# A hybrid decoder layer in split float32r: token parts of 688 and 344 instead of 516 and 516 in the Strassen products of the feed-forward block

## Chip, cores and metric

The kernel runs on one core of a Trainium2 chip. The metric is the time of one execution on the device in microseconds (us). Three runs of the kernel before the change took 2125.63, 2126.91 and 2134.8 us; the median is 2126.91 us.

## What is computed

One inference step of a one-layer decoder for 1024 prompt tokens and 8 sample tokens (1032 columns in all, `TOK`), width 1024. The time mixing (RWKV-7 and gated DeltaNet) fills the first half of the run and is not touched. What follows is, cut to its core:

```python
gate_a = jax.nn.sigmoid(pg[..., :D_MODEL])
gate_b = jax.nn.sigmoid(pg[..., D_MODEL:])
mix = gate_a * (o_a.astype(act) @ w_branch_a) + gate_b * (o_b.astype(act) @ w_branch_b)
h = h + mix @ w_out
u2 = rmsnorm(h, norm_ffn)
h = h + (jax.nn.silu(u2 @ w_ffn_gate) * (u2 @ w_ffn_up)) @ w_ffn_down
h = h + jax.nn.sigmoid(rmsnorm(h, norm_ple) @ w_ple_gate) * (pe.astype(act) @ w_ple_proj)
```

Weights are 1024x1024 for `w_out`, 1024x2816 for gate and up (22 tiles of 128, `NF`), 2816x1024 for down.

## The kernel before

Activations lie transposed: 128 features on the partitions, tokens in the columns. Every large product is made in float32r with both operands split in two: `x = xh + xl`, `w = wh + wl`, and for each 128x128 block of weights three products `wh*xh`, `wh*xl`, `wl*xh` (`mm`, L75). `wh` is made by ScalarE (ACT, L186), `wl` by GpSimd (POOL, L187) in `halves_of`, from raw weights that SyncE (SP) loads. `dense` takes one output tile `m`: it loads and splits the weights (`weights`) and then runs `products` over blocks of tokens, each into a PSUM tile `acc`, which `evac` reads.

`wst` holds raw weights (2 buffers), `wsp` split ones (6).

From L1497 on, the product with `wo` runs in two halves of the tokens, `t = 0` and `t = 1`, 516 tokens each, made of two quarters `QB` of 258 columns (`QW`). The evacuation adds the input (loaded into a tile `a`), stores `h` to DRAM, and `square` adds up squares: a square `c` by ACT, added to `sq` by POOL (L1458). After the last `m` the squares are summed over the partitions by two small products into `f` (L75), with `inv_rms` on VectorE (DVE) between them, which gives the norm `R` of the quarter.

Then `mixes` (L1473) scales `H` (L1482) and makes, from four quadrants (features 0 to 511 and 512 to 1023, first and second quarter of the half), the seven sums of Strassen's scheme: a sum `c` (L1490), its high part `xh` by ACT (L1492) and its low part `xl` (L1493). DVE and POOL take sums and low parts in turn. The temporaries `c` come from the same two buffers as the squares.

`strassen` (L1524) makes two output tiles of gate or up for a token half from seven products instead of eight: it loads four raw blocks of weights (`A_`, from a pool `raw` of 6 buffers), forms a sum of weights `s` for five of the seven (L1568; three on POOL, two on DVE), splits it, and multiplies by the matching sum of tokens: 12 `mm` of 258 columns per half. For the first pair of tiles (`f0 + j == 0`) gate and up run for half 0 alone and then again for half 1 (`for ts_ in ((0,), (1,))`), so their weights are loaded, summed and split twice. For the other ten pairs each split weight serves both halves. After 2, 4, 4, 4, 4, 4 tiles the down product runs (L1618), each block of 344 columns read from `h_d` into `a` (4 buffers), added (L1612) and stored back.

The pools `raw`, `sp`, `hid` of the feed-forward block are opened after `hpool.close()`, behind `mixes` of half 1:

```python
        XM.append(mixes(pool(cstk, f"xm{t}", 1, "right"), t, R))
    hpool.close()
    hstk = ExitStack()
    hp = pool(hstk, "hid")
    raw = pool(hstk, "raw", 6)
    sp = pool(hstk, "sp", 2)
```

They lie in the memory that `H`, `sq` and the halves of `mix` have left, so the first raw weights and sums of gate wait for the last use of those. A scheduler orders each engine's instructions by priorities (`tc.cur_priority`) and its own forecast of times; each engine then takes its instructions strictly in that order.

Of the kernel before, what the change touches and what calls it, by code (L numbers as in the profile page):

```python
# [58 lines left out]
def hybrid(ctx, tc, a, o):  # L59
# [120 lines left out]
    wst = pool(ctx, "wst", 2)  # L180
# [29 lines left out]
    def dense(src, nk, xh, xl, evac, blocks=range(NBLK)):  # L210

        tc.cur_priority += LATER
        wh, wl = weights(src, nk)
        tc.cur_priority -= LATER
        products(wh, wl, nk, xh, xl, evac, blocks)
# [3 lines left out]
    def products(wh, wl, nk, xh, xl, evac, blocks=range(NBLK), new=None):  # L219
        tc.cur_priority += LATER  # L220
        for b in blocks:
# [7 lines left out]
            for k in range(nk):  # L229
                mm(ps, wh[k], xh[k][:, c], start=(k == 0), stop=False)  # L230
                mm(ps, wh[k], xl[k][:, c], start=False, stop=False)
                mm(ps, wl[k], xh[k][:, c], start=False, stop=(k == nk - 1))
# [57 lines left out]
    with tc.tile_pool(name="ld", bufs=1, side="right", reuse_waits="tile") as ld, \  # L290
# [66 lines left out]
        def project(m):  # L357
            po = ld.tile([P, TOK], F32, tag="po", name="po", bufs=5)
# [1063 lines left out]

    def tile(tag, n=BW):
        return tmp.tile([P, n], F32, tag=tag, name=tag, bufs=4 if tag == "a" else 2)
# [8 lines left out]
    hpool, mstk = ExitStack(), ExitStack()  # L1433
    hq = pool(hpool, "hq", 1)
    H = [hq.tile([P, TOK], F32, name=f"H{m}") for m in range(KT)]
    mx = pool(mstk, "mx", 1)
    mh, ml = pair(mx, "mx", KT)
    for m in range(KT):
        def evac(b, ps, m=m):
            g = tile("a")  # L1440
            SP.dma_start(g, gate_d[KT + m, :, cols(b)])
            y = tile("c")
            stt(y, g, 1.0, ps, ADD, MULT)
            gtt(y, y, U[m][:, cols(b)], ADD)
            split(y, None, mh[m][:, cols(b)], ml[m][:, cols(b)])
        dense(a["wb"][m], HB, obh, obl, evac)
# [21 lines left out]
    QW = TOK // 4  # L1468
    QB = [slice(i * QW, (i + 1) * QW) for i in range(4)]
    cstk = ExitStack()  # L1470
    idr = diagonal(hq, QW)

    def mixes(pl_, t, R):  # L1473


        hi, lo = ([pl_.tile([P, 4, QW], F32R, name=f"x{q}{t}{i}") for i in range(7)] for q in "hl")
        tc.cur_priority += 2 * LATER
        for k in range(4):
            y = []
            for kk in (k, k + 4):  # L1480
                for c, r in zip(QB[2 * t:2 * t + 2], R):
                    stt(H[kk][:, c], H[kk][:, c], vc("nffn", kk), r, MULT, MULT)  # L1482
                    y.append(H[kk][:, c])
            y11, y12, y21, y22 = y
            for i, (p, q, op) in enumerate(((y11, y22, ADD), (y11, None, None), (y12, y22, SUB), (y21, y11, SUB),
                                            (y22, None, None), (y11, y12, ADD), (y21, y22, ADD))):
                e, e2 = (gtt, tt) if i % 2 else (tt, gtt)
                if op:
                    s = tile("c", QW)
# [4 lines left out]
        tc.cur_priority -= 2 * LATER  # L1494
# [3 lines left out]
    for t in range(2):  # L1498
        R = [hq.tile([P, QW], F32, name=f"R{t}{i}") for i in range(2)]
        sq = [hq.tile([P, QW], F32, tag=f"sq{i}", name="sq") for i in range(2)]  # L1500
        for m in range(KT):
            def evac(c, ps, m=m):
                i = (c.start - QB[2 * t].start) // QW
                x = tile("a", QW)
                SP.dma_start(x, a["xT"][m, :, c])
                h = H[m][:, c]
                tt(h, ps, x, ADD)
                SP.dma_start(h_d[m, :, c], h)
                square(m, c, h, sq[i], R[i], hq)
# [12 lines left out]
    sg = [hp.tile([P, TOK], F32, name=f"sg{i}") for i in range(2)]  # L1522

    def strassen(src, j, ts_, evac):  # L1524
# [3 lines left out]
        for i, q in ((0, 0), (1, 1), (1, 0), (0, 1)):  # L1528
            A_[i, q] = raw.tile([P, 4, P], F32, tag="r", name="r")
# [4 lines left out]
        def new(tag):  # L1534
            return sp.tile([P, QW], F32, tag=tag, name=tag)

        def sums(n, t, ps):
            if n == 0:
# [22 lines left out]
        for n, p, q, op, e in ((0, (0, 0), (1, 1), ADD, gtt), (3, (1, 1), None, None, None), (1, (1, 0), (1, 1), ADD, tt),  # L1561
                               (2, (0, 0), None, None, None), (4, (0, 0), (0, 1), ADD, gtt),
                               (5, (1, 0), (0, 0), SUB, tt), (6, (0, 1), (1, 1), SUB, gtt)):
# [5 lines left out]
            h, l = halves_of(s, 4)  # L1569
            for t in ts_:  # L1570
                banks.append(banks.pop(0))
                ps = banks[-1].tile([P, QW], F32, tag="acc", name="acc")
                xh_, xl_ = (x[n] for x in XM[t])
                for k in range(4):
                    mm(ps, h[:, k], xh_[:, k], start=(k == 0), stop=False)
                    mm(ps, h[:, k], xl_[:, k], start=False, stop=False)
                    mm(ps, l[:, k], xh_[:, k], start=False, stop=(k == 3))
                sums(n, t, ps)
            tc.cur_priority -= LATER

# [148 lines left out]
```

## Time and profile before

| | |
|---|---|
| median of three runs | 2126.91 us |
| the profiled execution | 2130.15 us, its span 2128.3 us |
| busy share of the span: PE, DVE, POOL, ACT | 91%, 62%, 50%, 40% |
| mean granted TensorE clock | 0.957 |
| chain that ended last | PE 62%, DVE 19%, POOL 5%, ACT 4%, DMA 4% |
| `mm` into `acc` in the chain | 53% of the span |

PE is the matrix engine's products, PEld its weight loads; DVE, ACT, POOL and SP are VectorE, ScalarE, GpSimd and SyncE. The duration of a product in a row is longer than its share of the time, since products are pipelined; what one costs is the distance from its start to the next start.

### The profile page before, as it was taken

Reading aid. Unit: us, or ns where it says so; the run is one execution under the profiler, and the core shown is the slowest. Engines: PE = TensorE matmul, PEld = TensorE weight load, DVE = VectorE, ACT = ScalarE, POOL = GpSimd, SP = SyncE. Lnnn points to the kernel's source line nnn. Section 1 sums busy time; section 2 is a strip of 40 time slices with the busy share of each in tenths; the row PEclk is TensorE's granted clock in tenths of the full one; section 3 lists DMA queues with packets and bytes.
Section 4 is the critical chain, followed back from the end, with each engine's and each line's share of the span. In section 5 each row is a group of like instructions: output and inputs, shape, how many; then the busy total and the mean of one; then the engine's idle time right before and its main releaser. Section 6 shows DMA issues by size and latency. Waiting matters only on the chain.

```text
span 2128.3 us, 40132 instructions
## 1 busy us (share of the span) xinstructions
PE 1936.3 (91%) x14676; PEld 1804.6 (85%) x14676; DVE 1328.3 (62%) x3264; ACT 856.3 (40%) x2080; POOL 1070.9 (50%) x1162
## 2 busy tenths in 40 slices
PE   6997999899899988999799908799999999999996
PEld 5987878777778868899799907699999999999995
DVE  8469756987898349636552756464463636446667
ACT  5343353555554341247423334242332414234542
POOL 5366362566563244741156559463554636455632
PEclk9999899999999999899899959999999999999998
DMA  6433332243343424554545511624335152432322
GB/s 218 143 110 106 105 106 87 83 127 94 98 126 113 147 83 122 165 154 137 167 138 168 149 35 60 214 61 147 113 96 164 61 170 79 136 110 79 94 92 96
DMA packets 215998, 252.96 MB, mean 119 GB/s; under 512 B 47960, under 2 KB 171752, under 8 KB 215800
## 3 DMA queue, kind: packets, MB, share of 16 engines
q1 hardware_dynamic: 215800, 250.39, 38.3%
q8 instruction: 115, 1.88, 0.4%
q14 instruction: 83, 0.68, 0.1%
HBM read 172.92 MB, written 77.40 MB: 118 GB/s over the span
## 4 chain that ended last, share of the span: by engine, by line
PE 62%; DVE 19%; POOL 5%; issue 5%; ACT 4%; DMA 4%; SPq 1%; DVEq 0%; ACTq 0%; POOLq 0%
PE acc L75 53%; PE f L75 3%; PE c L75 2%; POOL wl L187 2%; PE zp L75 1%; DVE GM L737 1%; DVE inv L773 1%; PE f L79 1%; DVE L L626 1%; DMA a<-h_d 1%; PE s L75 1%; POOL xl L1493 1%; PE x L75 1%; DMA ws<-in_wpg 1%; DVE LB L761 1%
## 5 line engine op out<-in xcount | busy, mean ns | idle before, releaser
L75 PE MATMUL acc<-xh,wh 128*128 128x258 f32 (+2 forms) x2360 | 733.8, 311 | 44.3 <-ACT wh L186 33.8
L75 PE MATMUL acc<-xl,wh 128*128 128x258 f32 (+2 forms) x2360 | 727.6, 308 | 1.3 <-DVE xl L253 1.3
L75 PE MATMUL acc<-xh,wl 128*128 128x258 f32 (+1 forms) x2336 | 722.5, 310 | 1.1 <-POOL wl L187 1.0
L75 PEld LDWEIGHTS acc<-xh,wh 128*128 128x128 f32 (+1 forms) x2360 | 450.5, 191 | 55.4 <-ACT wh L186 37.7
L187 POOL TENSOR_TENSOR wl<-ws,wh 128x512 fp32r<-128x512 f32 (+1 forms) x204 | 264.9, 1301 | 395.4 <-ACT wh L186 335.5
L75 PEld LDWEIGHTS acc<-xl,wh 128*128 128x128 f32 (+1 forms) x2360 | 451.5, 191 | 9.2 <-DVE xl L253 2.4
L75 PEld LDWEIGHTS acc<-xh,wl 128*128 128x128 f32 x2336 | 447.4, 192 | 8.0 <-POOL wl L187 2.2
L187 POOL TENSOR_TENSOR wl<-s,wh 128x512 fp32r<-128x512 f32 x120 | 157.1, 1313 | 154.6 <-ACT wh L186 149.5
L186 ACT ACTIVATE wh<-ws 128x512 fp32r<-128x512 f32 (+1 forms) x204 | 126.2, 620 | 206.2 <-PE acc L75 140.2
L75 PE MATMUL acc<-hidh,wh 128*128 128x344 f32 x528 | 165.9, 320 | 8.8 <-DVE a L1612 8.8
L75 PE MATMUL acc<-hidl,wh 128*128 128x344 f32 x528 | 168.4, 321 | 0.0
L75 PE MATMUL acc<-hidh,wl 128*128 128x344 f32 x528 | 167.3, 319 | 0.0
L1612 DVE TENSOR_TENSOR a<-a,acc 128x344 f32<-128x344 f32 x120 | 60.8, 512 | 148.4 <-DMA a<-h_d 92.4
L186 ACT ACTIVATE wh<-s 128x512 fp32r<-128x512 f32 x120 | 75.6, 630 | 142.1 <-PE acc L75 122.8
L75 PEld LDWEIGHTS acc<-hidh,wh 128*128 128x128 f32 x528 | 98.7, 188 | 10.3 <-DVE a L1612 5.6
L75 PEld LDWEIGHTS acc<-hidl,wh 128*128 128x128 f32 x528 | 99.0, 188 | 0.0
L75 PEld LDWEIGHTS acc<-hidh,wl 128*128 128x128 f32 x528 | 98.9, 188 | 0.0
L1568 POOL TENSOR_TENSOR s<-r 128x512 f32<-128x512 f32 x72 | 96.6, 1344 | 4.6
L187 POOL TENSOR_TENSOR wl<-r,wh 128x512 fp32r<-128x512 f32 x48 | 63.9, 1331 | 61.5 <-ACT wh L186 57.0
L492 POOL TENSOR_TENSOR cy<-cy,cu 128x344 f32<-128x344 f32 x72 | 68.6, 953 | 48.8 <-ACT cu L491 42.7
L75 PE MATMUL acc<-mxh,wh 128*128 128x258 f32 x256 | 72.7, 284 | 0.0
L75 PE MATMUL acc<-mxl,wh 128*128 128x258 f32 x256 | 72.4, 283 | 0.0
(496 smaller groups left out, 4143.5 us busy)
## 6 DMA issues: line engine op xcount, KB each, us to landing
ws<-in_win SPq DMA_DIRECT2D x92, 256.0 KB, 3.1
a<-h_d SPq DMA_DIRECT2D x120, 172.0 KB, 2.4
h_d<-a SPq DMA_DIRECT2D x120, 172.0 KB, 2.8
pa_d<-gs SPq DMA_DIRECT2D x90, 172.0 KB, 1.9
r<-in_wg SPq DMA_DIRECT2D x48, 256.0 KB, 2.7
r<-in_wu SPq DMA_DIRECT2D x48, 256.0 KB, 2.6
ws<-in_wd SPq DMA_DIRECT2D x40, 256.0 KB, 2.7
gate_d<-gs SPq DMA_DIRECT2D x48, 172.0 KB, 2.7
```

The source lines that it names most:

```text
L75: last[0] = TE.matmul(out, w, x, start=start, stop=stop).ins
L79: last[0] = TE.transpose(out, x, ident).ins
L186: act(h, s, AF.Copy)
L187: (eng or gtt)(l, s, h.bitcast(F32), SUB)
L492: gtt(y, y, u, ADD)
L626: V.tensor_tensor_scan(L[:, c * C:c * C + C], ones[:, 0:C], L[:, c * C:c * C + C], 0.0, MULT, ADD)
L737: stt(GM[:, 2 * (c + j) + h], ps[h][:, j], cvf[:, cg, h:h + 1], rwmask, MULT, MULT)
L761: V.transpose(LB[0:32, i0:i0 + 16], G2[:, :, i0:i0 + 16].rearrange("p b i -> p i b"))
L773: tt(u[:, :i], XB[:, :i, :i], LB[:, 16 + i:17 + i, 16:16 + i].to_broadcast([P, i, i]), MULT)
L1493: e2(lo[i][:, k], p, hi[i][:, k].bitcast(F32), SUB)
L1568: e(s, A_[p], A_[q], op)
L1612: tt(y, y, ps, ADD)
```

## The change

The two token parts get 688 and 344 tokens, each still of two equal blocks: 344 columns in part 0 and 172 in part 1. `H`, the norms `RN` and the halves of `mix` become one set of tiles for each part, `products` gets an offset `t0`. The sums in `mixes` get three buffers `ms` of their own, the scaling is one instruction per feature tile over the whole part, and the seven sums are made one after the other in the order in which they are used (`SIX`). The pools that Strassen uses (`sp`, `sx`, and `sg`) are opened ahead of the product with `wo`; the raw weights lie in `wst` (now 3 buffers) and `sp`. In the first pair gate takes all seven products of part 0 and then, with the same split weights, those of part 1; up is done as in the other pairs. `po` in the start goes from 5 buffers to 4, `a` from 4 to 3 before the down products and to 5 in them.

```diff
-    wst = pool(ctx, "wst", 2)
+    wst = pool(ctx, "wst", 3)
...
-            po = ld.tile([P, TOK], F32, tag="po", name="po", bufs=5)
+            po = ld.tile([P, TOK], F32, tag="po", name="po", bufs=4)
...
-        return tmp.tile([P, n], F32, tag=tag, name=tag, bufs=4 if tag == "a" else 2)
+        return tmp.tile([P, n], F32, tag=tag, name=tag, bufs=depth[0] if tag == "a" else 2)
...
+    QB = [slice(0, BW), slice(BW, 2 * BW), slice(2 * BW, 5 * BW // 2), slice(5 * BW // 2, TOK)]
+    NT_ = [2 * BW, BW]
...
+    sp, sx = pool(sstk, "sp", 2, "right"), pool(sstk, "sx", 1, "right")
+    sg = [sp.tile([P, TOK], F32, name=f"sg{i}", bufs=1) for i in range(2)]
+    SIX = (0, 3, 1, 2, 4, 5, 6)
...
-        tc.cur_priority += 2 * LATER
-        for k in range(4):
-            y = []
-            for kk in (k, k + 4):
-                for c, r in zip(QB[2 * t:2 * t + 2], R):
-                    stt(H[kk][:, c], H[kk][:, c], vc("nffn", kk), r, MULT, MULT)
...
+        tc.cur_priority += LATER
+        for m in range(KT):
+            stt(H[t][m], H[t][m], vc("nffn", m), RN[t], MULT, MULT)
+            y.append([H[t][m][:, :qw], H[t][m][:, qw:]])
+        for i in SIX:
+            for k in range(4):
...
                 if op:
-                    s = tile("c", QW)
+                    s = hq.tile([P, BW], F32, tag="ms", name="ms", bufs=3)[:, :qw]
...
-    hpool.close()
+    hstk0.close()
+    tstk.close()
     hstk = ExitStack()
+    tmp = pool(hstk, "tf", 2)
+    depth[0] = 5
     hp = pool(hstk, "hid")
-    raw = pool(hstk, "raw", 6)
-    sp = pool(hstk, "sp", 2)
...
-            A_[i, q] = raw.tile([P, 4, P], F32, tag="r", name="r")
+            A_[i, q] = (wst if i == q else sp).tile([P, 4, P], F32, tag="ws", name="ws")
...
+            h, l = halves_of(s, 4, sx if n == 6 else None)
+            part(n, 0, h, l)
+            if apart:
+                second.append((n, 1, h, l))
+            else:
+                part(n, 1, h, l)
+        for x in second:
+            part(*x)
...
-            for ts_ in ((0,), (1,)) if f0 + j == 0 else ((0, 1),):
-                strassen(a["wg"], f0 + j, ts_, gate)
-                strassen(a["wu"], f0 + j, ts_, up)
+            strassen(a["wg"], f0 + j, gate, f0 + j == 0)
+            strassen(a["wu"], f0 + j, up)
```

**Order on PE, behind the product with `wo`.** `mxh` and `mxl` are the halves of `mix`, `xh` and `xl` the sums of tokens with the part and the sum in their number (`xh06`: part 0, sum 6), `f` the small products of the norm, `wh` and `wl` split weights. Before:

```order
L75 MATMUL acc_14438<-mxh7_12507,wl_14378 128x258
L75 MATMUL f_14412<-c_14410,cs_75 128x258
L75 MATMUL f_14435<-nre_14415,cs_75 128x258
L75 MATMUL f_14469<-c_14467,cs_75 128x258
L75 MATMUL f_14492<-nre_14472,cs_75 128x258
L75 MATMUL acc_14659<-xh00_13711,wh_14655 128x258
```

With the change:

```order
L75 MATMUL acc_14466<-mxh17_12531,wl_14407 128x172
L75 MATMUL acc_14675<-xh00_13750,wh_14671 128x344
...
L75 MATMUL acc_14739<-xl02_13759,wh_14735 128x344
L75 MATMUL f_14441<-c_14439,cs_75 128x172
...
L75 MATMUL acc_14806<-xh06_13756,wl_14803 128x344
L75 MATMUL acc_14822<-xh10_14527,wh_14671 128x172
```

Four small products of the second part's norm stood between `wo` and the first product of gate; now gate's seven products of part 0 stand there, the norm's products among them, and part 1 takes up the same weights (`wh_14671`).

**Order on POOL, around the sums of part 0.** `sq<-sq,c` are the squares of the second part, `wl<-ws` weights of `wo`, `s` sums of weights of gate. Before:

```order
L1490 TENSOR_TENSOR c<-H_12492 128x258
L1493 TENSOR_TENSOR xl_13724<-c,xh_13717 128x258
L1458 TENSOR_TENSOR sq<-sq,c 128x258 x12
L1493 TENSOR_TENSOR xl_14510<-H_12493,xh_14503 128x258
...
L1493 TENSOR_TENSOR xl_14512<-c,xh_14505 128x258
L1568 TENSOR_TENSOR s<-r 128x512
```

With the change:

```order
L1507 TENSOR_TENSOR ms<-H_12505,H_12509 128x344
L187 TENSOR_TENSOR wl<-ws,wh 128x512
L1510 TENSOR_TENSOR xl_13760<-ms,xh_13753 128x344
L1473 TENSOR_TENSOR sq<-sq,c 128x172
L1507 TENSOR_TENSOR ms<-H_12507,H_12503 128x344
L1600 TENSOR_TENSOR s<-ws 128x512
L1473 TENSOR_TENSOR sq<-sq,c 128x172
L1507 TENSOR_TENSOR ms<-H_12509,H_12505 128x344
```

The second part's squares stood behind all sums of the first half, and the sums of gate's weights behind those of both; now all three alternate.

**Order on POOL in the start.** `pes<-pes` at the line of the final sums is the last sum of squares of a token block's first norm, `xs<-xs,R` its scaling, `wl<-ws` the first weights of the input projection. Before:

```order
L336 TENSOR_TENSOR pes<-pes 128x344 x2
L187 TENSOR_TENSOR wl<-ws,wh 128x512 x2
L336 TENSOR_TENSOR pes<-pes 128x344 x2
L338 TENSOR_TENSOR pes<-pes 128x344
L187 TENSOR_TENSOR wl<-ws,wh 128x512
L338 TENSOR_TENSOR pes<-pes 128x344
L354 TENSOR_TENSOR xs<-xs,R_327 128x344 x4
```

With the change:

```order
L337 TENSOR_TENSOR pes<-pes 128x344 x2
L187 TENSOR_TENSOR wl<-ws,wh 128x512 x3
L337 TENSOR_TENSOR pes<-pes 128x344 x2
L187 TENSOR_TENSOR wl<-ws,wh 128x512
L339 TENSOR_TENSOR pes<-pes 128x344
L355 TENSOR_TENSOR xs<-xs,R_327 128x344 x4
L187 TENSOR_TENSOR wl<-ws,wh 128x512
L339 TENSOR_TENSOR pes<-pes 128x344
```

Two more weight halves and a block's four scalings now stand ahead of the last sum of squares.

## Rows read from the trace of the kernel before

**Rows 1.** Span and mean granted TensorE clock of the only core.

```profile
core 0: 2128.3 us, clock 0.957
```

**Rows 2.** Busy time of each engine by stretch: bounds in us and length, then busy us (instructions) of PE, PEld, DVE, ACT, POOL, then the granted clock, the DMA share and GB/s. The stretches are the product with `wo`, the gap behind it, the first Strassen pair, the first down product, the five further groups up to the last down product, and the end.

```profile
1126.30:1220.80 94.50, 94.13 (x778) 93.52 (x776) 45.38 (x105) 33.13 (x70) 56.90 (x58) 1.00 0.58 164
1220.80:1281.60 60.80, 4.51 (x8) 2.17 (x8) 32.96 (x88) 21.86 (x54) 31.31 (x44) 0.54 0.10 32
1281.60:1335.10 53.50, 47.01 (x327) 42.96 (x327) 34.18 (x50) 26.32 (x55) 53.44 (x39) 0.95 0.22 70
1335.10:1374.10 39.00, 25.71 (x156) 23.70 (x154) 15.20 (x27) 7.33 (x16) 19.30 (x19) 1.00 0.72 218
1374.10:1960.40 586.30, 586.26 (x4512) 586.29 (x4513) 302.71 (x612) 208.41 (x449) 296.59 (x229) 1.00 0.35 110
1960.40:2128.30 167.90, 146.34 (x893) 140.72 (x891) 115.33 (x256) 64.65 (x133) 71.58 (x66) 0.94 0.32 104
```

**Rows 3.** Timeline of PE in three places with products in float32r that run back to back, of 258, 344 and 384 columns; the two rows of a place are the first and the last of 10, 5 and 6 starts in a row. Columns: start us, duration us, engine, line, operation, output<-operands, rows*columns of the weights, output shape, count.

```profile
1425.06 0.29 PE L75 MATMUL acc<-xh,wh 128*128 128x258 f32 x1
1426.14 0.28 PE L75 MATMUL acc<-xh,wh 128*128 128x258 f32 x1
...
1341.73 0.32 PE L75 MATMUL acc<-hidl,wh 128*128 128x344 f32 x1
1342.36 0.32 PE L75 MATMUL acc<-hidh,wl 128*128 128x344 f32 x1
...
2045.04 0.34 PE L75 MATMUL acc<-uxh,wh 128*128 128x384 f32 x1
2045.91 0.34 PE L75 MATMUL acc<-uxh,wl 128*128 128x384 f32 x1
```

**Rows 4.** Timeline of PEld (the weight loads), columns as in rows 3: two loads behind a wait, then the six loads of six products that are only 32 columns wide, and the next load.

```profile
1308.57 0.19 PEld L75 LDWEIGHTS acc<-xh,wh 128*128 128x128 f32 x1 [1.72 <-ACT wh L186]
1308.68 0.19 PEld L75 LDWEIGHTS acc<-xl,wh 128*128 128x128 f32 x1
...
744.90 0.79 PEld L75 LDWEIGHTS f<-sc,cs 128*128 128x128 f32 x6
745.61 0.19 PEld L75 LDWEIGHTS acc<-xl,wh 128*128 128x128 f32 x1
```

**Rows 5.** Timeline of PE: eight instructions of products in plain float32, 128 columns wide (two instructions make one such product), and what follows them.

```profile
939.93 1.06 PE L75 MATMUL o<-S,q 128*128 128x128 f32 x8
940.83 0.60 PE L79 MATMUL f<-cs,q 128*128 128x128 f32 x4
```

**Rows 6.** Who PE waited for from 1126 to 1375 us: us in total, times, longest.

```profile
PE acc L75 <- ACT wh L186: 33.8, 8, 27.8
PE f L75 <- DVE c L1464: 16.5, 1, 16.5
PE f L75 <- DVE nre L285: 12.4, 3, 8.0
PE acc L75 <- DVE a L1612: 12.4, 6, 3.5
```

**Rows 7.** Timeline of POOL behind the product with `wo`: last subtraction for the first half's sums, the additions of the second half's squares, and the first sum of weights of the first Strassen product.

```profile
1228.04 0.64 POOL L1493 TENSOR_TENSOR xl<-c,xh 128x258 fp32r<-128x258 f32 x1 [1.30 <-ACT xh L1492]
1228.64 8.28 POOL L1458 TENSOR_TENSOR sq<-sq,c 128x258 f32<-128x258 f32 x12
1279.48 1.44 POOL L1568 TENSOR_TENSOR s<-r 128x512 f32<-128x512 f32 x1
```

**Rows 8.** Groups of instructions on POOL from 1126.3 to 1335.1 us, shapes apart: busy us, mean ns of one | idle before, releaser.

```profile
L187 POOL TENSOR_TENSOR wl<-ws,wh 128x512 fp32r<-128x512 f32 x27 | 35.2, 1310 | 27.4 <-ACT wh L186 27.1
L1568 POOL TENSOR_TENSOR s<-r 128x512 f32<-128x512 f32 x13 | 17.9, 1387 | 0.0
L1458 POOL TENSOR_TENSOR sq<-sq,c 128x258 f32<-128x258 f32 x24 | 17.1, 732 | 4.8 <-ACT c L1456 4.8
L1493 POOL TENSOR_TENSOR xl<-c,xh 128x258 fp32r<-128x258 f32 x24 | 16.6, 707 | 13.2 <-ACT xh L1492 13.2
```

**Rows 9.** The same view of POOL over the whole span: the same kind of operation at 344 and at 128 columns.

```profile
L492 POOL TENSOR_TENSOR cy<-cy,cu 128x344 f32<-128x344 f32 x72 | 68.6, 953 | 48.8 <-ACT cu L491 42.7 <-DMA pa_d<-gs 5.8
L933 POOL TENSOR_TENSOR sx<-sS,sv 128x128 f32<-128x128 f32 x16 | 9.6, 602 | 0.6
```

**Rows 10.** Timeline of DVE: the eight scalings of the first half's second quarter by its norm, which start when that norm (`R`) is there.

```profile
1196.62 4.71 DVE L1482 SCALAR_TENSOR_TENSOR H<-H,vec,R 128x258 f32<-128x258 f32 x8 [0.95 <-ACT R L288]
```

**Rows 11.** The chain of waits through the first down product: start us, us, what. A load into a buffer of `a`, a store from it behind the addition, and the next load into it.

```profile
1350.78 2.63 DMA a<-h_d
1354.14 3.02 DMA h_d<-a
1357.17 3.30 DMA a<-h_d
```

**Rows 12.** The start: PE's longest wait before the first layer products, and on POOL a weight half, the last sum of squares (`pes`) and the scalings behind them.

```profile
40.78 0.65 PE L75 MATMUL acc<-ph,wph 128*128 128x344 f32 x1 [5.72 <-DVE po L363]
...
33.01 1.30 POOL L187 TENSOR_TENSOR wl<-ws,wh 128x512 fp32r<-128x512 f32 x1
34.26 0.94 POOL L338 TENSOR_TENSOR pes<-pes 128x344 f32<-128x344 f32 x1
35.14 3.52 POOL L354 TENSOR_TENSOR xs<-xs,R 128x344 f32<-128x344 f32 x4
```

More of the change, by code (lines that the diff above doesn't have):

```diff
@@ L208, in hybrid, with dense @@
     LATER = 100000
-    def dense(src, nk, xh, xl, evac, blocks=range(NBLK)):
+    def dense(src, nk, xh, xl, evac, blocks=range(NBLK), t0=0):
         tc.cur_priority += LATER
@@ L214, in dense, with products @@
         tc.cur_priority -= LATER
-        products(wh, wl, nk, xh, xl, evac, blocks)
+        products(wh, wl, nk, xh, xl, evac, blocks, t0=t0)
     banks = [psd]
-    def products(wh, wl, nk, xh, xl, evac, blocks=range(NBLK), new=None):
+    def products(wh, wl, nk, xh, xl, evac, blocks=range(NBLK), new=None, t0=0):
         tc.cur_priority += LATER
@@ L1432, in hybrid, with of @@
     astk.close()
[L1433 to L1437, printed above, removed]
+    QB = [slice(0, BW), slice(BW, 2 * BW), slice(2 * BW, 5 * BW // 2), slice(5 * BW // 2, TOK)]
+    NT_ = [2 * BW, BW]
+    hstk0, astk, mstk, m0stk = ExitStack(), ExitStack(), ExitStack(), ExitStack()
+    hq = pool(hstk0, "hq", 1)
+    H = [None, [hq.tile([P, NT_[1]], F32, name=f"H1{m}") for m in range(KT)]]
+    RN = [hq.tile([P, NT_[t]], F32, name=f"R{t}") for t in range(2)]
+    h0 = pool(astk, "h0", 1)
+    H[0] = [h0.tile([P, NT_[0]], F32, name=f"H0{m}") for m in range(KT)]
+    mx = [None, pool(mstk, "mx1", 1)]
+    mx[0] = pool(m0stk, "mx0", 1)
+    mh, ml = ([[mx[t].tile([P, NT_[t]], F32R, name=f"mx{q}{t}{m}") for m in range(KT)] for t in range(2)] for q in "hl")
+    def of(x, m, c):
+        t = int(c.start >= 2 * BW)
+        return x[t][m][:, c.start - 2 * BW * t:c.stop - 2 * BW * t]
     for m in range(KT):
@@ L1559, in sums, with part @@
                 evac(0, QB[2 * t], ps, t1[t])
-        for n, p, q, op, e in ((0, (0, 0), (1, 1), ADD, gtt), (3, (1, 1), None, None, None), (1, (1, 0), (1, 1), ADD, tt),
-                               (2, (0, 0), None, None, None), (4, (0, 0), (0, 1), ADD, gtt),
-                               (5, (1, 0), (0, 0), SUB, tt), (6, (0, 1), (1, 1), SUB, gtt)):
+        def part(n, t, h, l):
+            tc.cur_priority += LATER
+            banks.append(banks.pop(0))
+            ps = banks[-1].tile([P, width(QB[2 * t])], F32, tag="acc", name="acc")
+            xh_, xl_ = (x[n] for x in XM[t])
+            for k in range(4):
+                mm(ps, h[:, k], xh_[:, k], start=(k == 0), stop=False)
+                mm(ps, h[:, k], xl_[:, k], start=False, stop=False)
+                mm(ps, l[:, k], xh_[:, k], start=False, stop=(k == 3))
+            sums(n, t, ps)
+            tc.cur_priority -= LATER
+        second = []
+        for n, p, q, op, e in zip(SIX, ((0, 0), (1, 1), (1, 0), (0, 0), (0, 0), (1, 0), (0, 1)),
+                                  ((1, 1), None, (1, 1), None, (0, 1), (0, 0), (1, 1)),
+                                  (ADD, None, ADD, None, ADD, SUB, SUB), (gtt, None, tt, None, gtt, tt, gtt)):
             tc.cur_priority += LATER
@@ L1568, in strassen @@
                 e(s, A_[p], A_[q], op)
[L1569 to L1578, printed above, removed]
-            tc.cur_priority -= LATER
+            h, l = halves_of(s, 4, sx if n == 6 else None)
+            tc.cur_priority -= LATER
+            part(n, 0, h, l)
[5 more added lines that the diff above has]
+            part(*x)
     f0 = 0
@@ L1584, in gate @@
             def gate(i, c, ps, x):
-                y = sp.tile([P, QW], F32, tag="y", name="y", bufs=3)
+                y = sp.tile([P, BW], F32, tag="y", name="y")[:, :width(c)]
                 tt(y, ps, x, ADD)
@@ L1589, in up @@
             def up(i, c, ps, x, j=j):
-                y = sp.tile([P, QW], F32, tag="y", name="y", bufs=3)
+                y = sp.tile([P, BW], F32, tag="y", name="y")[:, :width(c)]
                 tt(y, ps, x, ADD)
@@ L1620, in hybrid @@
     hstk.close()
-    tstk.close()
     tmp = pool(ctx, "te", 2)
```

63 lines of the change are left out of this document (33 added, 30 removed).

## The prediction

> **What bounds the kernel now.** I read the span first: 2128.3 us on the one core [rows 1]; the page puts 62% of the chain that ended last on PE. Then a table of stretches around the change [rows 2], because a share over the whole run mixes stages with different limits. Three kinds of stretch are to be seen. In the product with `wo` and in the ten later Strassen pairs PE is busy without a break (94.13 of 94.5 us, 586.26 of 586.3): the time there is the number of products times the distance from one start to the next, and nothing that another engine gains can show. Between them PE stands almost still: 4.51 us busy of 60.8, at a granted clock of 0.54, and then 13.3 us are lost in 39.0 of the first down product. In the 53.5 us of the first pair POOL is the one that is full (53.44 busy) while PE has gaps.
>
> Who PE waited for there [rows 6]: 27.8 us for one split weight, 16.5 for the second half's squares, 12.4 for its norms, 12.4 for loads of `a`. POOL's rows tell why [rows 7]: the second half's squares come only behind the last sum of the first half (1228.64), and the first sum of gate's weights at 1279.48, behind the last sum of the second half, although its operands are loaded weights. Before the change that sum can't come earlier, as its memory is free only then.
>
> **The change, part by part.** Each sum below is against the profiled execution.
>
> *Narrow products, ten later pairs.* Two products of 258 columns become one of 344 and one of 172. Starts lie 1.08/9 = 0.120 us apart at 258 columns, 0.63/4 = 0.158 at 344, 0.87/5 = 0.174 at 384 [rows 3]. No row shows a float32r product of 172. From below, the straight line through these three (0.43 ns per column) gives 0.083. But each product loads its weights, and loads alone follow each other at 0.11 us even where the products have only 32 columns: 0.11 between two behind a wait, 0.71/6 = 0.118 for six [rows 4]; plain float32 instructions of 128 columns, each with its load, go at 0.90/8 = 0.112 [rows 5]. I take 0.112, the nearest row with a load for each instruction; 0.120, what 258 columns cost, is the dearer end of this reading. Twenty calls of `strassen` of 84 pairs of products: 1680 x (0.158 + 0.112 - 0.240) = +50 us (0.120: +64). The count is right: 3360 x 0.120 + 1152 x 0.158 = 585 us, the measured 586.3. All of it is on the path, since PE has no gap there.
>
> The rows say that a 172-column product pays for its load. The Trainium skill, TensorE: Matmul & The Clock Gate, section "Back-to-back issue gap", says otherwise: a stream of load and product pairs sustains about 81 ns at 128 columns and 131 at 512, so some 87 ns at 172 as an estimate; this term would then be +8 and the whole change -27 us. No row here shows a 128-column load under 0.11 us, so I stay with the rows.
>
> *From the first product with `wo` to the first down product*, 94.5 + 60.8 + 53.5 = 208.8 us now [rows 2]. PE's own work becomes 384 x (0.158 + 0.112) = 103.7 for `wo` and 168 x 0.270 = 45.4 for gate and up of the first pair, 149 in all: at best -60. If no part of the gap closes, the longer products alone make +14. Between these the order decides. Gate's products of part 0 now stand right behind `wo`, and what they wait for is POOL. The norm of the first half is in use 23 us after that half's last product (1196.62 [rows 10] less 1126.3 + 47.3), so after the change at 60.7 + 23 = 84 us from the start of `wo`. The scalings are as many elements as 2.67 times the eight of 4.71 us, 12.6 us on DVE at most; the first sums need five of eight: +92. From there POOL has in its queue, until the last split weight of up: part 0's 24 sums and low parts at 0.953 [rows 9] = 22.9; part 1's 24 and its 12 squares at 0.63, between 0.602 at 128 columns [rows 9] and 0.707 to 0.732 at 258 [rows 8], = 22.7; weights of gate and up, 14 x 1.31 + 6 x 1.39 [rows 8] = 26.7, where the four calls of before had twice that; four last weights of `wo`, 5.2. That is 77.5, so 169.5; the last products of up add 3.2, and I add 4 for POOL's waits for ACT (13.2 us for 24 of these now [rows 8]). 177 instead of 208.8: **-32 us**. The clock of 0.54 goes with the gap, and small products of the norm gain a little, which I leave out. What is late next is POOL: gate's products of part 0 come as fast as their weights and sums, not as fast as PE.
>
> *Buffers of `a`, 4 to 5, in the first down product.* A load, addition and store hold a buffer for 1357.17 - 1350.78 = 6.4 us [rows 11]; 24 blocks over 4 buffers are 38, over 5 they are 31, against 22.8 of PE work. DMA is already at 0.72 of its time [rows 2], so I take **-6** and leave 0 to -8 in the bounds. In the later down products PE is full, and the buffers change nothing. With 3 buffers in the branches a block of 12 products (1.9 us) leaves three blocks, 5.7 us, for a load, and loads into `a` take 2.63 us and more [rows 11]: hidden; if it were not, PE would show it at `a`.
>
> *The start.* On POOL two more weight halves of 1.30 us and four scalings of 3.52 now stand ahead of the last sum of squares: 6.1 us later [rows 12]. PE waited until 40.78 for another thing there, so part of that is covered. Bounds 0 and +6, taken at **+3**, the middle. The fourth buffer of `po` less and the third `wst` more act in the same place and are in these bounds.
>
> *Raw weights from 6 buffers of `raw` to 2 of `sp` and shares of `wst`*: nothing. In the later pairs POOL is busy half the time (296.59 of 586.3 [rows 2]) and a call lasts some 22 us, so loads have room. If the cover were gone, PE would wait for `wh` in these stretches.
>
> Sum: +50 - 32 - 6 + 3 = +15 us. The profiled execution took 2130.15, 3.2 above the median of the runs; a measurement tells some 0.5% (10.6 us) from no change. Against the median 2126.9 the forecast is **2142 us**, slower by 0.7%. Its own range runs from -60 for the gap (2114) to 0.120 for the narrow product and -10 for the gap (2178); most of it lies in 2125 to 2165.
>
> **Rivals.**
>
> *The narrow product costs its columns* (0.083). The two parts then cost as much as before (1680 x 0.001 = +2), and the closed gap is left: +2 - 32 - 6 + 3 = -33, 2094 us, faster. It decides at a distance of 0.100: there the first term is +30 and the sum about zero. The line of rows 3 speaks for it, rows 4 and 5 against. The rule of the skill above is of this kind, and would give 2100.
>
> *The narrow product falls to the rate of plain float32.* Nothing in float32r under 258 columns is to be seen, so a dearer price can't be excluded. A plain product of 128 columns is two instructions, 0.225 us [rows 5], 1.76 ns per column, or 0.302 at 172. Then 1680 x 0.220 = +370, and the first stretch is PE's: 60.7 + 116 + 77 = 254, +45. Sum +412, 2539 us. Rows 3 show no sign of a step between 384 and 258.
>
> *The gap stays under another name.* The squares of part 1 now stand between the sums of part 0 in POOL's queue; each waits for a product of `wo`, and the products of the second norm stand among gate's on PE. If part 0's sums are held up until `wo` is through, gate starts 25 us and more behind it, that stretch keeps its 209 us, and the sum is +47: 2174 us. For it speaks that POOL is the full engine there [rows 2]; against it that two squares are due every 48 x 0.112 = 5.4 us, with sums to fill the time.
>
> **How the numbers follow.** Forecast 0.67, columns alone 0.10, plain float32 rate 0.13, gap stays 0.10. Of the forecast's 0.67 I put 0.20 below +10.6 us (a larger part of the gap closed, the start unharmed) and 0.02 below -10.6. Faster: 0.10 + 0.02 = 0.12; same: 0.20; slower: 0.45 + 0.13 + 0.10 = 0.68. The range 2100 to 2180 holds the forecast with its bounds and the gap that stays, 0.77, and the edge of the first rival; the plain rate and most of the columns' case are left out.
>
> **What would show it.** Products into `acc` of 172 columns 0.112 us apart and those of 344 at 0.158; the ten later pairs with their down products at 636 us instead of 586; gate's first product within a few us of the last of `wo`, with no stretch of 10 us without PE; the first down product some 177 us behind the first product of `wo`; POOL full between these. I am wrong if 172 columns cost under 0.100 or over 0.130, if PE waits for `wh` in the later pairs, or if it stands still over 25 us behind `wo`.

## The result, and the profile after

| | kernel before | changed kernel |
|---|---|---|
| median of the runs, us | 2129.44 (2125.63 to 2134.8, 4 runs) | 2151.53 (2146.48 to 2154.83, 4 runs) |
| profiled execution, us | 2130.15 | 2146.48 |
| its span, us | 2128.3 | 2144.7 |

The changed kernel takes 1.010 times as long, with a 95% interval of 1.007 to 1.013: slower by 22 us at the medians, where 2142 us, 15 more than before, had been forecast.

Four stretches tell where the time went. The table of stretches of the changed kernel, with columns as in [rows 2]; the first row is everything ahead of the product with `wo`, the second that product, the next four the first Strassen pair, then the first down product, the five further groups, and the end.

```profile
0.00:1119.70 1119.70, 1025.74 (x8010) 911.33 (x8011) 781.13 (x2127) 495.83 (x1310) 538.64 (x710) 0.96 0.41 126
1119.70:1226.60 106.90, 106.00 (x778) 104.89 (x776) 48.92 (x88) 35.44 (x71) 68.15 (x60) 1.00 0.48 142
1226.60:1250.00 23.40, 15.06 (x61) 13.17 (x61) 18.69 (x31) 11.54 (x26) 22.67 (x21) 0.70 0.20 59
1250.00:1272.00 22.00, 10.23 (x35) 8.21 (x33) 20.58 (x49) 7.79 (x21) 11.76 (x14) 0.66 0.06 19
1272.00:1292.00 20.00, 19.74 (x94) 19.44 (x95) 14.96 (x28) 10.86 (x31) 19.41 (x26) 0.54 0.11 33
1292.00:1313.00 21.00, 21.00 (x161) 21.00 (x160) 12.37 (x29) 7.69 (x20) 8.00 (x9) 1.00 0.30 89
1313.00:1344.40 31.40, 27.35 (x171) 25.91 (x170) 14.91 (x26) 6.33 (x12) 15.18 (x13) 1.00 0.77 239
1344.40:1976.80 632.40, 632.40 (x4488) 632.40 (x4489) 305.89 (x613) 203.47 (x448) 296.17 (x231) 1.00 0.34 103
1976.80:2144.70 167.90, 146.17 (x892) 140.80 (x891) 116.83 (x254) 64.28 (x131) 69.59 (x64) 0.95 0.32 101
```

Against [rows 2]: the later pairs went from 586.3 to 632.4 us, +46.1. From the first product with `wo` to the first down product it was 208.8 and is 1313.0 - 1119.7 = 193.3, -15.5. The first down product went from 39.0 to 31.4, -7.6; the end stayed at 167.9. That is +23.0, and the medians say +22.1. The boundary between two of these is not the same in both kernels: 24 products of the later pairs, 12 of each width and 3.2 us of PE's time, stand inside the 31.4 us (4488 of PE's instructions come behind it, 4512 before the change). With these counted where they belong, the later pairs take 635.6 us, +49.3, and the first down product 28.2, -10.8. Ahead of `wo` the profiled execution was 6.6 us shorter (1119.7 for 1126.3), but in eleven kernels of the experiments, with practically the same work up to there, `wo` began anywhere between 1121.7 and 1142.2, so I give it no meaning.

PE's timeline in the later pairs, as in [rows 3]: the first and the last of twelve starts at 344 columns and of eleven at 172.

```profile
1349.76 0.32 PE L75 MATMUL acc<-xh,wh 128*128 128x344 f32 x1
...
1351.49 0.32 PE L75 MATMUL acc<-xh,wl 128*128 128x344 f32 x1
...
1351.73 0.28 PE L75 MATMUL acc<-xl,wh 128*128 128x172 f32 x1
...
1352.85 0.27 PE L75 MATMUL acc<-xh,wl 128*128 128x172 f32 x1
```

1.73/11 = 0.157 us and 1.12/10 = 0.112 us: a product of 172 columns, half as wide, is only a little cheaper.

Who PE waited for from 1226 to 1313 us, the answer to [rows 6]:

```profile
PE acc L75 <- DVE xl L1510: 6.4, 3, 3.8
PE acc L75 <- ACT wh L186: 6.1, 3, 2.8
PE f L75 <- DVE nre L286: 4.7, 1, 4.7
```

The waits of 27.8 us for a weight and of 16.5 for the squares are gone. What is left are waits of a few us, among them one for the second norm (`nre`). PE's timeline between 1282 and 1286 us, the first and the last of sixteen starts, shows what came in their place: products of part 1 that are 3.20/15 = 0.213 us apart, not 0.112. The granted clock there is 0.5, the lower of the two levels (1.2 GHz).

```profile
1282.62 0.42 PE L75 MATMUL acc<-xl,wh 128*128 128x172 f32 x1
...
1285.82 0.42 PE L75 MATMUL acc<-xh,wl 128*128 128x172 f32 x1
```

### The profile page after: what moved, and what is told of

It is laid out like the page before. It is cut to its first block, busy times and chain, and to the rows that moved or that the text cites. A ratio compares the mean times of both kernels' runs of the same rounds, so it can differ in the third digit from the quotient of the medians.

```text
span 2144.7 us, 40063 instructions
## 1 busy us (share of the span) xinstructions
PE 2003.7 (93%) x14676; PEld 1877.2 (88%) x14676; DVE 1334.3 (62%) x3240; ACT 843.2 (39%) x2068; POOL 1049.6 (49%) x1142
## 3 DMA queue, kind: packets, MB, share of 16 engines
q1 hardware_dynamic: 214648, 248.29, 37.8%
## 4 chain that ended last, share of the span: by engine, by line
PE 68%; DVE 20%; DMA 3%; issue 3%; ACT 3%; POOL 3%; SPq 0%; DVEq 0%; POOLq 0%; ACTq 0%
PE acc L75 59%; PE f L75 3%; PE c L75 2%; DVE GM L738 1%; DVE inv L774 1%; PE zp L75 1%; PE f L79 1%; DVE inv L775 1%; PE s L75 1%; PE x L75 1%; DVE inv L776 1%; DVE L L627 1%; DVE LB L762 1%; DVE H L1497 1%; DMA a<-h_d 1%
## 5 line engine op out<-in xcount | busy, mean ns | idle before, releaser
L75 PE MATMUL acc<-xh,wh 128*128 128x344 f32 (+2 forms) x2360 | 753.1, 320 | 10.5 <-ACT wh L186 6.1
L75 PE MATMUL acc<-xl,wh 128*128 128x344 f32 (+2 forms) x2360 | 751.3, 319 | 6.6 <-DVE xl L1510 6.4
L75 PE MATMUL acc<-xh,wl 128*128 128x344 f32 (+1 forms) x2336 | 746.0, 320 | 1.3 <-POOL wl L187 1.3
L187 POOL TENSOR_TENSOR wl<-ws,wh 128x512 fp32r<-128x512 f32 (+1 forms) x248 | 321.1, 1297 | 463.5 <-ACT wh L186 433.1
L186 ACT ACTIVATE wh<-ws 128x512 fp32r<-128x512 f32 (+1 forms) x248 | 153.7, 622 | 248.5 <-PE acc L75 213.5
L187 POOL TENSOR_TENSOR wl<-s,wh 128x512 fp32r<-128x512 f32 x110 | 142.9, 1300 | 160.9 <-ACT wh L186 160.7
L1600 POOL TENSOR_TENSOR s<-ws 128x512 f32<-128x512 f32 x66 | 86.3, 1307 | 32.5 <-DMA ws<-in_wg 13.7
L75 PE MATMUL acc<-mxh,wl 128*128 128x344 f32 (+1 forms) x256 | 76.4, 298 | 0.9 <-POOL wl L187 0.9
L1622 DVE TENSOR_TENSOR y<-y,sg 128x344 f32<-128x344 f32 x88 | 75.2, 854 | 3.0
L75 PE MATMUL acc<-mxl,wh 128*128 128x344 f32 (+1 forms) x256 | 76.4, 298 | 0.0
```

The costliest lines, as they stand in the source:

```text
L75: last[0] = TE.matmul(out, w, x, start=start, stop=stop).ins
L186: act(h, s, AF.Copy)
L187: (eng or gtt)(l, s, h.bitcast(F32), SUB)
L1600: e(s, A_[p], A_[q], op)
L1622: tt(y, y, sg[i][:, c], MULT)
```

## The experiments

"Stretch" is short for the time from the first product with `wo` to the first down product: 208.8 us before, 193.3 after. It is read from one profiled execution of each kernel. Kernels that do the same work in it agree to 0.3 us: 193.3 and 193.4 (the changed kernel and the one with half weights), 175.8 and 176.1 (equal parts with five and with four buffers of `a`).

### Equal parts, the rest of the change kept

```diff
-    QB = [slice(0, BW), slice(BW, 2 * BW), slice(2 * BW, 5 * BW // 2), slice(5 * BW // 2, TOK)]
-    NT_ = [2 * BW, BW]
+    QW = TOK // 4
+    QB = [slice(i * QW, (i + 1) * QW) for i in range(4)]
+    NT_ = [2 * QW, 2 * QW]
```

> The changed kernel with equal parts again (516 and 516 tokens, blocks of 258), all else of the change kept: own buffers, order of the sums, the first gate pair's weights kept for both parts, buffers of a. My theory (width is what the change loses by, the order is what it gains by): products of 258 columns 0.120 us apart, ten later pairs with their down products back at 586 us (from 632), wo at 95 us (from 107), first wo product to first down product about 180 us (193 after, 209 before), total about 2095 us (2085 to 2105), 1.5% below the kernel before. Rival (the gap behind wo closes because the parts are unequal): the first stretch stays at 205 us or more, total about 2125 us, level with the kernel before.

Measured: 2088.49 us, 0.979 (0.975 to 0.983) of the kernel before. It beats both kernels. Its stretches: `wo`, the first pair in two rows, the first down product, the five further groups.

```profile
1127.20:1220.80 93.60, 93.60 (x777) 93.38 (x776) 48.48 (x95) 37.97 (x82) 65.88 (x65) 1.00 0.59 168
1220.80:1261.00 40.20, 19.11 (x94) 16.51 (x93) 35.59 (x75) 15.77 (x38) 27.57 (x29) 0.73 0.09 30
1261.00:1303.00 42.00, 35.92 (x253) 34.11 (x253) 31.65 (x58) 19.79 (x51) 31.52 (x34) 0.89 0.21 63
1303.00:1335.10 32.10, 26.02 (x145) 25.10 (x146) 14.27 (x27) 4.54 (x9) 11.66 (x10) 0.89 0.70 217
1335.10:1921.20 586.10, 586.10 (x4511) 586.10 (x4510) 302.49 (x611) 211.84 (x451) 301.02 (x231) 1.00 0.37 112
```

The later pairs are back at 586.1, and the stretch is 1303.0 - 1127.2 = 175.8, 33 less than before. So the loss is the widths, and the gap behind `wo` does not need unequal parts to close: they cost 17.5 us in the stretch and 635.6 - 586.1 = 49.5 in the later pairs.

### Other widths: what sets the price of a narrow product

Edits: the same lines with `QW` and the narrow width 300 and 216, then 368 and 148.

> The changed kernel with parts of 600 and 432 tokens (blocks of 300 and 216 columns). Floor theory (a narrow float32r product pays 0.112 us whatever its columns): 216 columns at 0.112, 300 at about 0.139, a pair 0.251 instead of 0.270; later pairs about 600 us instead of 632, total about 2112 us. Rival (the narrow product costs its columns at a dearer rate, 0.65 ns each as 172 at 0.112 would have it): 216 columns at 0.141, the pair 0.280, later pairs about 649 us, total about 2170 us.

> The changed kernel with parts of 736 and 296 tokens (blocks of 368 and 148 columns). Floor theory: 148 columns again at 0.112, 368 at about 0.168, a pair 0.280; later pairs about 649 us. Rival (cost in proportion to the columns below some width, 0.65 ns each): 148 columns at 0.096, the pair 0.264, later pairs about 622 us. The third reading, columns alone at the slope of the wide products (0.43 ns), would give 0.073.

Measured: 2111.21 us (0.990 of before, 0.987 to 0.994) and 2187.66 us in a single run. The later pairs took 600.8 and 653.7 us. By the floor 600 and 649 were expected, both counted from 632, which lacks the 24 products; from 635.6 they are 603.7 and 652.4. PE's timeline of the first of these kernels, then of the second: first and last of five starts in a row of the narrow product (then eight) and of eleven of the wide one.

```profile
1400.68 0.27 PE L75 MATMUL acc<-xl,wh 128*128 128x216 f32 x1
...
1401.13 0.27 PE L75 MATMUL acc<-xh,wl 128*128 128x216 f32 x1
...
1401.38 0.30 PE L75 MATMUL acc<-xl,wh 128*128 128x300 f32 x1
...
1402.77 0.29 PE L75 MATMUL acc<-xh,wl 128*128 128x300 f32 x1
```

```profile
1450.20 0.28 PE L75 MATMUL acc<-xl,wh 128*128 128x148 f32 x1
...
1450.98 0.28 PE L75 MATMUL acc<-xh,wl 128*128 128x148 f32 x1
...
1451.31 0.33 PE L75 MATMUL acc<-xl,wh 128*128 128x368 f32 x1
...
1452.99 0.33 PE L75 MATMUL acc<-xh,wl 128*128 128x368 f32 x1
```

216 columns are 0.45/4 = 0.112 us apart, 148 columns 0.78/7 = 0.111; 300 take 1.39/10 = 0.139 and 368 take 1.68/10 = 0.168. It is a floor: 148, 172 and 216 columns all cost the same.

### Half the weights to load

```diff
-                mm(ps, h[:, k], xl_[:, k], start=False, stop=False)
+                mm(ps[a_], h[:, k, a_], xl_[:, k], start=False, stop=False)
```

with `a_` the first 64 columns for eight of the twelve products of a block.

> The changed kernel with half weights in two calls (up of the fourth and sixth pairs): of the twelve part 1 products of each block, eight load and use only the first 64 columns of their weight tile (rows 64 to 127 of the output get fewer terms, so part of the sum is left out). Load theory (0.112 us is the load of 128 weight columns): the products with 64 columns come closer together, at 0.083 to 0.09 us, where their 172 columns are the limit. Rival (a floor of the float32r product itself, whatever the load): still 0.112 us apart.

Measured: 2148.68 us in a single run. PE's timeline in the fourth pair: three products with a whole weight tile, eight with half of one, one whole.

```profile
1507.24 0.28 PE L75 MATMUL acc<-xl,wh 128*128 128x172 f32 x1
1507.35 0.27 PE L75 MATMUL acc<-xh,wl 128*128 128x172 f32 x1
1507.46 0.24 PE L75 MATMUL acc<-xh,wh 128*64 128x172 f32 x1
...
1508.02 0.24 PE L75 MATMUL acc<-xl,wh 128*64 128x172 f32 x1
1508.10 0.28 PE L75 MATMUL acc<-xh,wl 128*128 128x172 f32 x1
```

With half a tile to load the same 172 columns come 0.56/7 = 0.080 us apart. So the floor goes with the 128 columns of the weight tile, and below it the price by columns (0.083 by the line through [rows 3]) holds. The load of the tile is the likely reason, since products of only 32 columns with a whole tile come 0.118 us apart too [rows 4]; but the edit also halves the width of the product's output, and no run parts the two. The Trainium skill, TensorE: Matmul & The Clock Gate, section "LDWEIGHTS (loading the stationary operand)", gives a load as the weight's columns over 1.2, so 107 ns for 128 and 53 for 64: the trace agrees (0.112 us; and 0.080 at 64, above the 53 ns). The 81 ns of that page's section "Back-to-back issue gap", for a sustained product of 128 columns, are below what these float32r products show with a load of 128 columns.

### More products in the gaps, to hold the clock

```diff
+                if apart and t == 0:
+                    for _ in range(5):
+                        mm(fill, h[:, k], xh_[:, k], start=True, stop=True)
```

> The changed kernel with 140 products more: behind each of the 28 steps of the first gate pair's part 0, five products of 344 columns into a spare bank that nobody reads, so that PE is busy where it waited for sums. Clock theory (part of the expected gain of the order was lost because PE ran part 1's gate products at the 1.2 GHz level after its gaps): the granted clock stays at or near 1.00 from 1230 to 1290 us, part 1's gate products come 0.112 us apart instead of 0.213, and the first wo product to the first down product takes about 185 us instead of 193; total some 8 us lower, 2140 to 2146, though PE does 22 us more work. Rival (PE only follows what DVE and POOL feed it, the clock costs nothing): the stretch stays at 193 us or grows by up to 10.

Measured: 2158.61 us (1.012, 1.010 to 1.015), stretch 192.7. The rows that answer to 1250 to 1313 us:

```profile
1263.00:1290.20 27.20, 22.87 (x131) 22.58 (x130) 23.30 (x56) 10.90 (x27) 14.78 (x18) 0.87 0.05 15
1290.20:1305.00 14.80, 13.58 (x98) 13.12 (x97) 12.14 (x22) 8.47 (x24) 13.91 (x19) 0.88 0.06 19
```

Part 1's gate now starts 1290.2 - 1133.3 = 156.9 us behind the first product with `wo` (152.1 without fill, at 1271.8), since the fill itself held PE up. From there it is 35.8 us to the first down product instead of 41.2, and part 1's gate products are 0.112 us apart instead of 0.213, as the clock theory said. First and last of seventeen starts:

```profile
1290.21 0.28 PE L75 MATMUL acc<-xl,wh 128*128 128x172 f32 x1
...
1292.00 0.27 PE L75 MATMUL acc<-xh,wl 128*128 128x172 f32 x1
```

The clock gave back 5.4 us and the fill took 4.8. The granted clock came to 0.87 and 0.88, not to 1.00, and neither 185 us nor a lower total was reached, so the stretch by itself does not tell the theories apart.

### The second norms cut short, then both

```diff
-                square(m, c, h, sq[i], RN[t][:, i * qw:i * qw + qw], hq)
+                square(m, c, h, sq[i], RN[t][:, i * qw:i * qw + qw], hq, steps=(3, 0)[t])
```

> The changed kernel with the three Newton steps of the inverse root left out for part 1's two norms behind wo (18 small DVE instructions of some 42; part 1 is scaled by the rough first guess). DVE theory (part 1's gate products wait for the second norms, a serial chain on DVE that my POOL queue did not hold): part 1's scaling starts some 10 us earlier, first wo product to first down product falls from 193 to about 183 us, total about 2141. POOL theory (my forecast: POOL's queue of 77 us sets the end): stays within 3 us of 193.

> The changed kernel with the Newton steps of part 1's two norms left out, as in e8_short_norm, and with 92 products more that nobody reads in the gaps of the first gate pair (none in its first two blocks, then 1, 5, 5, 6 and 6 behind each step), fewer and later than in e4_fill. Two-cause theory (the second norms on DVE and the half clock behind the gaps end at about the same time, so that either alone taken away shows nothing): granted clock near 1.00 from 1250 to 1290 us, part 1's gate products begin some 145 us behind the first wo product and come 0.112 apart, first wo product to first down product about 182 us instead of 193. POOL theory (POOL's queue sets the end whatever PE and DVE do): stays at 190 us or more.

> The changed kernel with the 92 later fill products alone, norms whole. Two-cause theory: part 1's gate products still begin at about 152 us behind the first wo product, but run at the full clock: the stretch falls from 193 to about 187 us. POOL theory: 190 us or more.

Measured: short norms 2160.33 us (1.014, 1.010 to 1.017), stretch 193.4; late fill alone 2159.14 us (1.012, 1.008 to 1.016), stretch 194.9; both 2148.32 us (1.007, 1.004 to 1.009), stretch 185.4. Short norms alone, DVE's timeline at the scalings of part 1:

```profile
1259.93 6.98 DVE L1497 SCALAR_TENSOR_TENSOR H<-H,vec,R 128x344 f32<-128x344 f32 x8
```

The stretches behind, of the same kernel:

```profile
1250.00:1272.30 22.30, 13.41 (x42) 10.57 (x43) 20.98 (x39) 8.24 (x25) 15.67 (x14) 0.58 0.05 18
1272.30:1292.30 20.00, 18.88 (x82) 17.99 (x80) 10.62 (x18) 6.56 (x19) 15.77 (x21) 0.50 0.06 20
```

Late fill alone, the 24 us that hold the wait for the second norm and the 19 that follow:

```profile
1262.00:1285.60 23.60, 15.92 (x85) 15.61 (x84) 19.78 (x52) 8.55 (x22) 10.85 (x13) 0.84 0.05 17
1285.60:1305.00 19.40, 18.80 (x92) 18.64 (x92) 15.66 (x26) 8.99 (x26) 18.67 (x25) 0.58 0.00 1
```

Both:

```profile
1250.00:1276.80 26.80, 24.16 (x142) 23.34 (x141) 24.59 (x48) 13.04 (x31) 22.05 (x22) 0.94 0.08 25
1276.80:1314.60 37.80, 34.60 (x253) 33.92 (x252) 29.94 (x57) 17.59 (x51) 27.21 (x34) 0.95 0.22 67
```

Each stretch is the start of part 1's gate behind the first `wo` product and what is left from there:

| | part 1's gate starts, us | from there to the first down product, us |
|---|---|---|
| changed kernel | 152.1 | 41.2 |
| short norms | 147.8 | 45.5 |
| late fill | 154.2 | 40.7 |
| both | 147.6 | 37.8 |

Short norms bring the scaling 9.5 us forward (135.4 us behind the first `wo` product, 144.9 without) and part 1's gate 4.3, and nothing of it is left at the end: the clock stands at 0.50 for the next 20 us. The 183 us of the DVE theory did not come. The late fill did not do what it was made for, as PE still had to wait for the norm and the clock fell behind that (0.58), so the 187 us did not come either. With both, the clock stays at 0.94 and the stretch loses 7.9 us. For the two together the two-cause theory held, though it had said 182. The POOL theory, which was my forecast's, had named the right stretch for either alone, but it fell with both, since POOL has the same work there.

### The first gate pair

```diff
-            strassen(a["wg"], f0 + j, gate, f0 + j == 0)
-            strassen(a["wu"], f0 + j, up)
+            for ts_ in ((0,), (1,)) if f0 + j == 0 else ((0, 1),):
+                strassen(a["wg"], f0 + j, gate, ts_)
+                strassen(a["wu"], f0 + j, up, ts_)
```

> e1_equal_parts with the first pair as in the kernel before: gate and up of part 0, then gate and up of part 1, with the weights loaded, summed and split twice; own buffers and the order of the sums stay. Theory A (kept weights carry the gain, 26.7 us of POOL's queue): first wo product to first down product grows from 176 us by 15 to 25, total about 2108. Theory B (own buffers and the order of the sums carry it): it grows by 0 to 8, total 2088 to 2096, and the gap of 60.8 us without PE stays closed.

and, the other way, with `strassen(a["wg"], f0 + j, gate)` for all pairs:

> e1_equal_parts with the first gate pair not taken apart: part 1's product stands behind part 0's for each weight, as in all other pairs, and the weights are still summed and split once. Queue theory (what matters is that POOL sums and splits these weights once): first wo product to first down product within 5 us of 176. Order theory (gate's part 0 must run ahead of part 1, since part 1's sums are not there): PE waits at the first part 1 product, the stretch grows by over 8 us, total 2097 or more.

Two passes: 2111.57 us (0.989, 0.986 to 0.992), stretch 193.2, 17.4 more than 175.8: theory A. Not apart: 2088.10 us (0.979, 0.976 to 0.982), stretch 176.9: that the parts stand one behind the other is worth nothing, that the weights are loaded, summed and split once is. From 208.8 to 175.8 the kept weights thus bring 17.4, and the other 15.6 come with the rest of the change: the buffers and the order of the sums, which were not tried apart. With two passes POOL is busy for 84 of the 99.5 us between the last product with `wo` and the first down product, and PE for 61:

```profile
1221.30:1320.80 99.50, 61.10 (x334) 55.91 (x333) 79.19 (x128) 40.45 (x97) 83.95 (x79) 0.74 0.15 48
```

### Buffers of `a`, and the start

```diff
-    depth[0] = 5
+    depth[0] = 4
```

> e1_equal_parts with 4 buffers of a in the down products instead of 5. Buffer theory: the first down product takes about 38 to 39 us instead of 32, as 24 blocks over 4 buffers of 6.4 us, and the later down products stay. Rival (the DMA queues at 0.77 of their time set it): within 2 us of 32.

```diff
-    wst = pool(ctx, "wst", 3)
+    wst = pool(ctx, "wst", 2)
-            po = ld.tile([P, TOK], F32, tag="po", name="po", bufs=4)
+            po = ld.tile([P, TOK], F32, tag="po", name="po", bufs=5)
```

> The equal parts of e1_equal_parts with the two buffer counts of the start put back: wst 2 instead of 3, po 5 instead of 4. Theory (the later start is these counts, and PE carries it to the end): first input-projection product at about 51 us instead of 59, total some 6 us under e1's 2088, about 2082. Rival (the start is covered, or two wst buffers cost it back in the later pairs): first product early but total within 3 us of 2088, or PE waits for split weights in the later pairs (over 2 us there).

Four buffers: 2107.44 us in a single run (its profiled span is 17.3 us over that with five, 15.0 of them ahead of `wo`, in the spread there), the first down product 34.2 us, 2.1 more than with five: near the rival, and far from the 38 of the buffer theory. The start put back: 2090.16 us (0.979, 0.977 to 0.982), level with equal parts. The first product of the layer's input came at 51.0 us instead of 58.8, but `wo` began at 1123.9 instead of 1127.2, inside the spread, and the medians show nothing: the start is covered.

## Why the prediction was right, point by point, and where it was not

*Narrow products, +50: right.* 0.112 and 0.158 us as taken, +49.3 in the later pairs like for like, with PE full (632.40 of 632.4). The floor at 148 and 216 columns and its fall with half a weight tile show that a narrow product pays for its weight tile and not for its own columns, as the reason had it. The rivals "columns alone" and "plain float32 rate" are out.

*First product with `wo` to first down product, -32: half of it came (-15.5). This is the step that failed.* In my sum POOL's queue set the end. Its last subtraction for `up` ended at 1292.95 + 2.56 = 1295.5, 175.8 us behind the first `wo` product, near the 173.5 forecast with the waits, but that is in part luck: it had begun at 83.2 instead of 92, its operations took 84 us instead of 77.5, and it stood still for 10.9 us in five waits. So it was not full (11.76 of 22.00 us from 1250 to 1272), and when it had finished PE was not 3.2 but 17.5 us from done. For 177 us part 1's gate had to start at 145, since behind its start PE had 168 products of 172 columns and 84 of 344 to do, 168 x 0.112 + 84 x 0.158 = 32 us at full clock. It started at 152.1, 7 us later, and from there it took 41.2 us, 9 more. Two terms were missing.

First, the second norm. My sum held 23 us from part 0's last product to its norm in use (that one came, part 0's scaling starting 79.3 us behind the first `wo` product where 84 was forecast), and nothing for part 1's norm. From the last `wo` product at 1226.34 to part 1's scaling at 1264.62 it took 38 us, and PE waited 4.7 us for this norm. DVE was full there (20.58 of 22.00). Its timeline, with POOL's beside it, shows the norm's steps on two numbers per partition:

```profile
1245.89 1.20 DVE L242 TENSOR_SCALAR nrr<-nrr 128x2 int32<-128x2 int32 x1
...
1251.16 1.20 DVE L246 SCALAR_TENSOR_TENSOR nrr<-nrr 128x2 f32<-128x2 f32 x1
1252.39 0.16 DVE L244 TENSOR_TENSOR nrr<-nrr 128x2 f32<-128x2 f32 x1
...
1264.62 1.55 DVE L1497 SCALAR_TENSOR_TENSOR H<-H,vec,R 128x344 f32<-128x344 f32 x3 [0.78 <-ACT R L289]
```

```profile
1245.80 1.27 POOL L187 TENSOR_TENSOR wl<-s,wh 128x512 fp32r<-128x512 f32 x1
...
1251.07 1.26 POOL L1600 TENSOR_TENSOR s<-ws 128x512 f32<-128x512 f32 x1
...
1292.95 2.56 POOL L187 TENSOR_TENSOR wl<-s,wh 128x512 fp32r<-128x512 f32 x2
```

A step takes 0.16 us when POOL is idle and up to 1.25 when one of POOL's large operations runs: in the two pairs of rows shown both end within 0.1 us of each other. Before the change the second half's norms had POOL idle beside them, and every step, on three numbers per partition there, took 0.16 or 0.17 us; first and last of nine on DVE, and POOL's next operation with its 18.81 us of idle time:

```profile
1240.11 0.16 DVE L243 TENSOR_TENSOR nrr<-nrr 128x3 f32<-128x3 f32 x1
...
1241.69 0.16 DVE L245 SCALAR_TENSOR_TENSOR nrr<-nrr 128x3 f32<-128x3 f32 x1
...
1255.73 1.63 POOL L1493 TENSOR_TENSOR xl<-H,xh 128x258 fp32r<-128x258 f32 x2 [18.81 <-ACT xh L1492]
```

The Trainium skill, SBUF — State Buffer, section "SBUF: two separate sides", calls the port pair that the two share an exclusive lock, held for a whole instruction; the trace agrees. So POOL's sums, moved up beside DVE's serial chain, make that chain longer: the 24 steps of the two norms took 4.0 us in all before and 12.3 with the change, 8.3 of the 38. What the end would be without that was not tried by itself.

Second, the clock. "The clock of 0.54 goes with the gap" was wrong: waits of up to 4.7 us were left, and from 1272 to 1292 the granted clock was again 0.54 with PE busy 19.74 of 20.00 us. 94 products took 20 us there; the next 21 us, at 1.00, held 161. The 9 us too many behind part 1's start are about what part 1's 84 gate products cost at 0.213 instead of 0.112 (8.5). Each cause hid the other, as the runs with short norms and fill show; both together are 7.9 us. Of the other 8 to the forecast's 177, 2.6 lie ahead of part 1's gate even with both (147.6 for 145) and 5.8 behind it (37.8 for 32); what they come from was not tried.

*First down product, -6: more came (-10.8 like for like, outside the bounds of 0 to -8), and the reason holds for a small part.* PE's waits for `a` fell from 12.4 us [rows 6] to 3.4, but four instead of five buffers cost only 2.1 us at equal parts. Before the change the last twelve products of the first pair, with a wait of 1.0 us for their weight, stood inside the 39.0, some 2.4 us. What the rest is was not tried.

*Start, +3: nothing of it reaches the end. Raw weights, 0: right*, no wait for `wh` in the later pairs.

*"The gap stays under another name": out.* The first gate product stands 3 us behind the last of `wo`, and the longest time without PE is 4.7 us.

```profile
1229.37 0.66 PE L75 MATMUL acc<-xh,wh 128*128 128x344 f32 x1 [2.75 <-ACT wh L186]
```

The sum said +15 and the stretches give +23: the failed term was 16.5 us off, and the first down product (4.8), the start (3) and the narrow products (0.7) were too dear. That these made up for half of it was luck, and it is why the total came so near; the failed term by itself stayed inside its bounds of -60 to -10.

## What to carry to other kernels

A float32r product that loads its own 128 weight columns had a floor in time here, so split a width equally, or keep both pieces above the floor: the line through [rows 3] meets 0.112 us at some 240 columns (172 + 0.029/0.00043), and a narrower piece pays for columns that it does not have. When a gap between two stages is closed by letting sums run earlier, write down three ends, not one: the queue of the engine that makes them, the serial chain that the last ones wait for, and the matrix engine's own work behind that chain, at the clock it will have after the waits that stay. And try the parts of a change apart: here one part gained 2% and another lost 3%.

## What was not expected of the hardware

- At the lower clock level products of 172 columns come 0.213 us apart and at the upper 0.112; the floor goes with the clock.
- A DVE instruction on two numbers per partition took up to 1.25 us beside a large POOL operation, 0.16 without: two serial chains of twelve took 12.3 us where they had taken 4.0.
- Two causes worth 7.9 us together showed next to nothing in the total when either was taken away alone: the stretch of 193.3 us became 193.4 with short norms, 192.7 or 194.9 with fill, and 185.4 with both. The start of part 1's gate told more: short norms brought it 4.3 us forward and the lower clock took the same back; the first fill sped up what lies behind it by 5.4 and put it 4.8 later by its own work.
